# Tying VectorE, ScalarE and all of TensorE to source order through the first MLP's half units

## The chip, the cores and the metric

The kernel runs on one core of a Trainium2 chip. The time is the device time of one execution in microseconds (us); the number compared is the median over several executions.

## The reference, cut to what matters

The reference is a decoder trunk of two layers for 256 rows of width 2048 in float32. Layer 0 mixes with banded attention, layer 1 with a gated linear recurrence; each layer ends with a squared-ReLU MLP. Every sub-layer starts with an RMS norm, whose result is shifted and scaled by vectors that come from a conditioning vector c, and ends with a gated residual.

```python
def modulate(h, shift, scale):
    return h * (1.0 + scale[:, None, :]) + shift[:, None, :]
...
def swa_sink_attention(h, w_in, w_out, q_gain, k_gain, sinks):
    proj = h @ w_in
...
    return out.reshape(B, T, ATTN_Q_DIM) @ w_out
...
def squared_relu_mlp(h, w1, w2):
    a = jax.nn.relu(h @ w1)
    return (a * a) @ w2
```

The change reaches from the start of the kernel through layer 0's attention and through the first part of its MLP's up projection (2048 of 8192 columns). What follows, from the down projection of layer 0 to the end, is not touched by it.

## The kernel before, in words

**Weights.** All weights stream from memory in pieces of 1 MB, called raws (128 x 2048 float32), loaded by SyncE (L212) into a ring of five buffers (`NRAW`). `prep_one` (L225) handles the next raw of a list `seq` fixed in the source. There are three kinds. An "m" raw is one column block of the modulation weights: VectorE multiplies it with c and sums along the row (L233). A "g" raw is a quarter of a group of four such blocks, computed by TensorE (`gemv`). A "w" raw is a weight of a matrix product: it is split in two halves of 128 x 1024, each of which ScalarE casts to a rounded value `wh` (L250) and VectorE turns into the rest `wl` (L251). The halves have five buffers (`NW`).

**One unit.** A product is computed as high times high, low times high and high times low, in float32r. One "w" raw makes a unit of 16 x 3 matmuls of 256 columns, 48 in all. After each unit the source calls `ahead(LAG - 1)` (L309), which casts and splits the weight of the unit after the next one, with the "m" and "g" raws that stand before it in `seq`. A raw's buffer is loaded anew when its cast and split are done.

**The operands.** The left operand `h` or `o` of a product is made per block of 128 columns by `make_h` (L543): VectorE scales X into `ht` (L547), ScalarE adds the shift and rounds it (L551), VectorE makes the low part (L552). `mod_prep` (L531, L539) makes the scale `gsc` for it. `make_u` (L561) does the same without the norm and the shift (L564, L565 on ScalarE, L566 on VectorE).

**The stages of layer 0 here.** First the norm of X with its `gemv` matmuls for the first four shift blocks, then the first four `h`. Then the in projection of attention in four quarters (`mm_quarter`), each of which needs four more `h`; ten partial sums per quarter are copied out by ScalarE (L851 for the first quarter, L846 for the next two) and added up by GpSimd. In the fourth quarter the attention steps begin (`step`, L819): per-head norms of q and k go through a chain of small VectorE operations (`rsqrt`, L132 to L138), are widened by VectorE (`widen`, L662) and spread by TensorE (tile `rbk`). The out projection follows; residual units are added to X by L581.

**`open_mlp` (L882).** Its list `order` has eight residual units and then four that alternate with "u" units, then the last u units, eight u units in all. A u unit (`mm_uhalf`) multiplies the first eight blocks of X, not yet normed, with half of an up weight; its result is put into `part` (L926), its shift sums into `sums` (L925). In the meantime the squares of X are summed (L498, L499), and the norm comes out as `rbs`. Then the remaining eight operands are made (`more_h` in the loop over k), and a loop of eight p's runs the second half of the same weights: `mm_half(H, 1, ev)`, where `ev` scales `part` (L940), adds both halves (L948), applies squared ReLU (L967) and rounds the result (L476, L477), and `more_h(p, p + 1)` makes one more `h` for later. The results of all eight p's are the operands of the down projection.

**What sets the order.** The source's calls pass through Tile's scheduler, which places the instructions of each engine. Within an engine it may put them in another order than the source's. Only TensorE's calls go through the class `Queue` (L42); those made by `pep` are pinned, which means that each is tied behind the TensorE instruction that stands before it in the source. VectorE and ScalarE are plain engine objects. Work delayed by `later(n, ...)` is run by `hook` at the n-th slot after it in the source, with slots inside the units' matmul loops. On the chip an engine carries out its instructions in the order in which they were placed.

Of the kernel before, what the change touches and what calls it, by code (L numbers as in the profile page):

```python
# [41 lines left out]
class Queue:  # L42


    def __init__(self, tc, engine, last, pin):
        self.tc, self.engine, self.last, self.pin = tc, engine, last, pin

    def __getattr__(self, name):
        fn = getattr(self.engine, name)

        def call(*args, **kw):
            r = fn(*args, **kw)  # L52
            if self.pin and self.last:
                self.tc.add_manual_dep(
                    r.ins, self.last[-1],
                    mybir.DependencyInfo(mybir.DependencyClass.NoSync, mybir.DependencyReason.DATA),
                    reason="issue order")
            self.last[:] = [r.ins.name]
            return r
        return call  # L60
# [2 lines left out]
@with_exitstack  # L63
def trunk(ctx, tc, a, out):
    nc = tc.nc
    dve, act, sp, pool_q = nc.vector, nc.scalar, nc.sync, nc.gpsimd
    last = []
    pe, pep = Queue(tc, nc.tensor, last, False), Queue(tc, nc.tensor, last, True)

# [249 lines left out]
    def later(delay, fn):  # L319
        bg.append((bgst["slot"] + delay, bgst["n"], fn))  # L320
        bgst["n"] += 1
        bg.sort(key=lambda e: (e[0], e[1]))

    def hook():
        bgst["slot"] += 1
        while bg and bg[0][0] <= bgst["slot"]:
            bg.pop(0)[2]()
# [15 lines left out]
    def mm_std(op, evac, count=1, fold=False):  # L343
        keys = list(range(st["w"], st["w"] + count))
        ahead(count - 1)
        pss = [mmtile() for _ in keys]
        for kb in range(KB):
            while op[kb] is None:
                fill[0]()
            for i, key in enumerate(keys):  # L350
                wh, wl = wtile(key, kb)
                if fold:
                    three(pss[i][:, :T], wh, wl, op[kb], kb == 0, kb == KB - 1)
                else:
                    pe.matmul(pss[i], lhsT=wh, rhs=op[kb][:, :2 * T], start=(kb == 0), stop=False)
                    pe.matmul(pss[i][:, :T], lhsT=wl, rhs=op[kb][:, :T], start=False,
                              stop=(kb == KB - 1))
                if (kb * count + i) % 4 == 3:
                    hook()
        for i, key in enumerate(keys):  # L360
            evac(pss[i])
            W.pop(key)
        st["w"] += count
        ahead(LAG - 1, False)
# [102 lines left out]
    def wt(cols=T, name="w"):  # L467
        return tmp.tile([P, cols], F32, tag="w", name=name, bufs=3)
# [23 lines left out]
    def norm_add(kb):  # L492
        if kb == 0:
            nstate["ss"] = tmp.tile([P, T], F32, tag="rbs", name="ssum", bufs=1)
            act.activation(out=nstate["ss"], in_=X[kb], func=AF.Square)
            return
        sq = wt()
        act.activation(out=sq, in_=X[kb], func=AF.Square)  # L498
        dve.tensor_tensor(out=nstate["ss"], in0=nstate["ss"], in1=sq, op=ALU.add)  # L499

    def norm_rstd(sumcol=ones[:, :1]):
        ss = psum.tile([P, 2], F32, tag="sp", name="sst", bufs=2)
        for b in range(2):
            pe.matmul(ss[:, b:b + 1], lhsT=nstate["ss"][:, b * P:(b + 1) * P], rhs=sumcol,
                      start=True, stop=True)
        sm = tmp.tile([P, 8], F32, tag="nsm", name="nsm")
        dve.tensor_scalar(out=sm[:, 0:2], in0=ss, scalar1=1.0 / D, scalar2=EPS,
                          op0=ALU.mult, op1=ALU.add)
        rsqrt(sm[:, 0:2], sm[:, 2:4], sm[:, 4:6], sm[:, 6:8])
        dg = tmp.tile([P, T], F32, tag="dg", name="dg", bufs=1)  # L510
        for b in range(2):
            dve.tensor_scalar(out=dg[:, b * P:(b + 1) * P], in0=ident, scalar1=sm[:, 2 + b:3 + b],
                              scalar2=None, op0=ALU.mult)
        nstate["dg"] = dg

    def norm_bcast():
        rb = psum.tile([P, T], F32, tag="sp", name="rb", bufs=2)
        pe.matmul(rb, lhsT=ones, rhs=nstate["dg"], start=True, stop=True)
        rbs = tmp.tile([P, T], F32, tag="rbs", name="rbs", bufs=1)
        act.copy(out=rbs, in_=rb)  # L520
        return rbs
# [21 lines left out]
    def make_h(l, half, rbs, kb, s):  # L543
        sh = SH1 if half == 0 else SH2
        g = l * 2 + half
        t = tmp.tile([P, T], F32, tag="ht", name="ht", bufs=2)
        dve.scalar_tensor_tensor(out=t, in0=X[kb], scalar=gsc[:, g, kb:kb + 1], in1=rbs,  # L547
                                 op0=ALU.mult, op1=ALU.mult)
        shc = mods[:, l, sh * 16 + kb: sh * 16 + kb + 1]
        h = optile(sets[s], kb)  # L550
        act.activation(out=h[:, :T], in_=t, func=AF.Identity, bias=shc)  # L551
        dve.scalar_tensor_tensor(out=h[:, T:2 * T], in0=t, scalar=shc, in1=h[:, :T].bitcast(F32),  # L552
                                 op0=ALU.add, op1=ALU.subtract)
        return h
# [29 lines left out]
    def evac_res(l, which, n):  # L584
        def f(ps):
            resid(l, which, n, ps)
            finish_x(n)
        return f
# [3 lines left out]
    def finish_x(n):  # L592
        if ustate["next"] is not None and n < ustate["lim"]:
            ustate["U"][n] = make_u(*ustate["next"], n)
        if n < KB - 1:
            later(2, lambda: norm_add(n))
        elif ustate["next"] is None:
            norm_add(n)
# [283 lines left out]
    def open_mlp(mp, A, relu2):  # L882
        for n in range(4):
            finish_x(n)
        parts, H, box = [], [None] * KB, {}
        sums = mp.tile([P, KB], F32, tag="sums", name="sums")

        def more_h(k0, k1):
            for k in range(k0, k1):
                H[k] = make_h(0, 1, box["rbs"], k, 0)  # L890

        def s2():
            box["rbs"] = norm_bcast()

        def s1():
            norm_rstd()
            later(NB, s2)

        def s0():
            norm_add(KB - 1)  # L900
            later(1, s1)

        def res(n):
            mm_std(O, evac_res(0, G1, n), fold=True)
            if n == KB - 1:
                later(1, s0)

        for i, (kind, n) in enumerate(order):
            if i == NO:
                prep_mods(0, SC2, KH)  # L910
                prep_mods(0, SH2, KH)
                mod_prep(0, 1, 0, KH)
                start_u(0, 1, KH)
                U = ustate["U"]
                for k in range(KH):
                    U[k] = make_u(0, 1, k)
            if kind == "o":
                res(n)
                continue
            part = mp.tile([P, 2 * T], F32, tag=f"acc{n}", name=f"part{n}")  # L920
            parts.append(part)

            def keep(u, ps):
                c = 2 * n + u
                dve.tensor_reduce(out=sums[:, c:c + 1], in_=ps[:, T:T + 2], axis=AX.X, op=ALU.add)  # L925
                act.copy(out=part[:, u * T:(u + 1) * T], in_=ps[:, :T])  # L926
            mm_uhalf(U, keep)
        while "rbs" not in box:
            hook()
        ustate["next"], ustate["lim"] = None, KB  # L930
        sets.reverse()
        for k in range(KH, KB, 2):
            prep_mods(0, SC2, k + 2)
            prep_mods(0, SH2, k + 2)
            mod_prep(0, 1, k, 2)
            more_h(k, k + 2)
        ahead(LAG - 1, False)
        for p in range(8):
            t2 = wt(2 * T)
            dve.tensor_tensor(out=t2.rearrange("p (a b) -> p a b", b=T),  # L940
                              in0=parts[p].rearrange("p (a b) -> p a b", b=T),
                              in1=box["rbs"].unsqueeze(1).to_broadcast([P, 2, T]), op=ALU.mult)

            def ev(ps):
                for u in range(2):
                    t = t2[:, u * T:(u + 1) * T]
                    n = 2 * p + u
                    dve.scalar_tensor_tensor(out=t, in0=ps[:, u * T:(u + 1) * T], scalar=sums[:, n:n + 1],  # L948
                                             in1=t, op0=ALU.add, op1=ALU.add)
                    relu2(A, n, t)  # L950
            mm_half(H, 1, ev)
            more_h(p, p + 1)
        return H

    def mlp_layer(l, H, last):
# [399 lines left out]
```

## Time and profile before

| | us |
|---|---|
| median of 3 executions | 2356.22 |
| lowest and highest | 2351.72, 2356.53 |
| the profiled execution | 2348.51 |
| its span | 2346.7 |

The profiled execution has 1.8 us around its span and lies 7.7 us below the median. Times inside it are counted from the span's start. The first 42 us are setup and the first norm, 42 to 173 us the first three quarters of attention's in projection, 173 to 333 us the fourth quarter, the attention and the start of its out projection, 333 to 451 us the residual and u units of `open_mlp`, 451 to 497 us its loop over p; from 497 us on the down projection runs. In rows of the profile, all TensorE instructions carry the line of the `Queue` class (L52), so they are told apart by the tile's name: `mm` is a product's accumulator, `rbk` the spread norm of q and k, `gt` the turned `gemv` result. A row of the timeline gives start, duration, engine, line, operation and names; a figure in brackets at its end is the idle time before it and what ended it.

### The profile page before, as it was taken

The numbers are of one execution on the slowest core, as the hardware profiler recorded it, in microseconds if no ns is written. First come the engines' busy times: TensorE is split into PE (matmuls) and PEld (weight loads), VectorE is DVE, ScalarE is ACT, GpSimd is POOL, SyncE is SP. The second block draws the span as 40 slices with busy tenths as digits, with TensorE's granted clock in tenths as the row PEclk, the third lists the DMA queues.
The fourth block names the chain that finished last, engine by engine and source line by source line (L and its number), as shares of the span: only waits on it lengthen the run. The fifth ranks groups of instructions, "written<-read, shape, count | busy, mean of one in ns | idle before, by whom it ended". The sixth has DMA issues, their size and how long they took to land.

```text
span 2346.7 us, 37064 instructions
## 1 busy us (share of the span) xinstructions
PE 2269.6 (97%) x14690; PEld 1992.0 (85%) x14690; DVE 1788.2 (76%) x2908; ACT 1163.1 (50%) x1962; POOL 100.7 (4%) x94
## 2 busy tenths in 40 slices
PE   5887899999999999999999999999999999999999
PEld 3775579998888888888888898899888888888888
DVE  5668679975888898897998888767865766665665
ACT  3344454544444444455666666655544444444443
POOL 0133530000000000000000000000000000000000
PEclk8999999999999999999999999999999999999999
DMA  9886799756898899985577777645666666655552
GB/s 361 310 305 257 272 335 341 253 195 215 323 336 323 327 333 324 334 317 187 196 284 267 259 267 268 214 164 180 231 233 231 236 227 239 207 189 186 191 194 94
DMA packets 84638, 598.80 MB, mean 255 GB/s; under 512 B 9457, under 2 KB 11505, under 8 KB 12273
## 3 DMA queue, kind: packets, MB, share of 16 engines
q1 hardware_dynamic: 81936, 593.81, 70.3%
q8 instruction: 115, 1.88, 0.3%
q10 hardware_dynamic: 2304, 2.10, 0.3%
q0 software_dynamic: 224, 0.52, 0.1%
q14 instruction: 59, 0.48, 0.1%
HBM read 594.04 MB, written 2.10 MB: 254 GB/s over the span
## 4 chain that ended last, share of the span: by engine, by line
PE 92%; DVE 4%; ACT 2%; DMA 1%; issue 1%; POOL 0%; ACTq 0%; SPq 0%; DVEq 0%; POOLq 0%
PE mm L52 89%; ACT wh L250 1%; DVE raw L233 1%; PE A L52 1%; DVE wl L251 1%; PE on L52 0%; PE S L52 0%; POOL h L771 0%; DVE asm L751 0%; DMA raw<-in_aoutk_dram 0%; DMA raw<-in_mod_w_dram 0%; PE cb L52 0%; PE pt L52 0%; DVE h L552 0%; PE pv L52 0%
## 5 line engine op out<-in xcount | busy, mean ns | idle before, releaser
L251 DVE TENSOR_TENSOR wl<-raw,wh 128x1024 fp32r<-128x1024 f32 x744 | 909.3, 1226 | 429.7 <-ACT wh L250 427.9
L250 ACT CAST wh<-raw 128x1024 fp32r<-128x1024 f32 x744 | 778.4, 1050 | 850.9 <-PE mm L52 773.2
L52 PE MATMUL mm<-h,wh 128*128 128x512 f32 (+2 forms) x3728 | 1155.4, 368 | 35.1 <-ACT wh L250 34.6
L52 PE MATMUL mm<-h,wl 128*128 128x256 f32 (+1 forms) x3232 | 908.9, 282 | 1.5 <-DVE wl L251 1.4
L52 PE MATMUL mm<-o,wh 128*128 128x512 f32 (+2 forms) x3120 | 860.4, 346 | 0.2 <-ACT h L759 0.2
L52 PEld LDWEIGHTS mm<-h,wh 128*128 128x128 f32 x3728 | 671.5, 190 | 161.9 <-ACT wh L250 39.0
L52 PE MATMUL mm<-o,wl 128*128 128x256 f32 (+1 forms) x2432 | 679.2, 280 | 0.0
L52 PEld LDWEIGHTS mm<-h,wl 128*128 128x128 f32 x3232 | 612.2, 190 | 11.1 <-issue 3.4
L52 PEld LDWEIGHTS mm<-o,wh 128*128 128x128 f32 x3120 | 539.9, 189 | 82.3 <-issue 2.5
L52 PEld LDWEIGHTS mm<-o,wl 128*128 128x128 f32 x2432 | 457.9, 188 | 0.7 <-issue 0.3
L233 DVE CUSTOM_DVE_ANT_0 raw<-raw,cond 128x2048 f32<-128x2048 f32 x160 | 365.7, 2286 | 9.5 <-DMA raw<-in_mod_w_dram 9.3
L52 PE MATMUL mm<-wh,h 128*128 128x256 f32 x576 | 105.9, 283 | 4.2 <-DVE h L552 2.7
L52 PEld LDWEIGHTS mm<-wh,h 128*128 128x128 f32 x576 | 88.8, 188 | 8.0 <-DVE h L552 3.2
L52 PE MATMUL mm<-wl,h 128*128 128x256 f32 x288 | 81.0, 281 | 0.0
L472 ACT COPY w<-mm 128x256 f32<-128x256 f32 x186 | 68.1, 366 | 0.0
L771 POOL TENSOR_SCALAR h<-h,asm 128x128 f32<-128x128 f32 x64 | 64.6, 1027 | 69.7 <-DVE asm L754 21.1
L476 ACT CAST h<-w 128x256 fp32r<-128x256 f32 x125 | 49.8, 403 | 23.9 <-DVE w L967 23.0
L52 PEld LDWEIGHTS mm<-wl,h 128*128 128x128 f32 x288 | 54.3, 188 | 0.5 <-issue 0.4
L967 DVE SCALAR_TENSOR_TENSOR w<-w 128x256 f32<-128x256 f32 x125 | 52.0, 421 | 2.2
L477 DVE TENSOR_TENSOR h<-w,h 128x256 fp32r<-128x256 f32 x125 | 51.5, 417 | 0.0
L473 DVE TENSOR_TENSOR w<-mm,w 128x256 f32<-128x256 f32 x109 | 45.6, 418 | 0.4 <-ACT w L472 0.2
L988 DVE TENSOR_TENSOR acc<-mm,acc 128x256 f32<-128x256 f32 x96 | 40.5, 422 | 6.3 <-PE mm L52 3.8
(203 smaller groups left out, 1134.6 us busy)
## 6 DMA issues: line engine op xcount, KB each, us to landing
raw<-in_mod_w_dram SPq DMA_DIRECT2D x160, 1024.0 KB, 5.5
raw<-in_mlp_dram SPq DMA_DIRECT2D x128, 1024.0 KB, 4.9
raw<-in_hin_dram SPq DMA_DIRECT2D x64, 1024.0 KB, 5.0
raw<-in_mlp1b_dram SPq DMA_DIRECT2D x64, 1024.0 KB, 4.8
raw<-in_mlp1a_dram SPq DMA_DIRECT2D x48, 1024.0 KB, 5.2
raw<-in_mod_g_dram SPq DMA_DIRECT2D x32, 1024.0 KB, 6.1
raw<-in_ainq_dram SPq DMA_DIRECT2D x20, 1024.0 KB, 6.8
raw<-in_m1h_dram SPq DMA_DIRECT2D x16, 1024.0 KB, 5.1
```

Of the source, the lines that this page charges most:

```text
L52: r = fn(*args, **kw)
L233: dve.tensor_tensor_reduce(out=r, in0=r, in1=cond, scale=1.0, scalar=0.0, op0=ALU.mult, op1=ALU.add, accum_out=mods[:, e[1], e[2]:e[2] + 1])
L250: act.copy(out=wh, in_=part)
L251: dve.tensor_tensor(out=wl, in0=part, in1=wh.bitcast(F32), op=ALU.subtract)
L472: act.copy(out=t, in_=ps[:, T:])
L473: dve.tensor_tensor(out=out_t, in0=ps[:, :T], in1=t, op=ALU.add)
L476: act.copy(out=opt[:, :T], in_=src_t)
L477: dve.tensor_tensor(out=opt[:, T:2 * T], in0=src_t, in1=opt[:, :T].bitcast(F32), op=ALU.subtract)
L771: pool_q.tensor_scalar(out=Ls[hh][:, cut[b]], in0=Ls[hh][:, cut[b]], scalar1=ri[:, i:i + 1], scalar2=None, op0=ALU.mult)
L967: dve.scalar_tensor_tensor(out=t, in0=t, scalar=0.0, in1=t, op0=ALU.max, op1=ALU.mult)
L988: dve.tensor_tensor(out=acc[n], in0=ps[:, :T], in1=acc[n], op=ALU.add)
```

## The change

`Queue` gets a class flag `strict`. While it is set, every instruction called through a `Queue`, pinned or not, is tied behind the instruction that its own engine got before it from the source, by a dependency that sets the order only and adds no semaphore. VectorE and ScalarE now are `Queue` objects of their own, so the rule holds for them, too. The flag is set at the start of the trunk and cleared at the end of `open_mlp`, that is, before layer 0's down projection; from there on the scheduler places as before.

```diff
 class Queue:
+    strict = True
...
         def call(*args, **kw):
             r = fn(*args, **kw)
-            if self.pin and self.last:
+            if (self.pin or Queue.strict) and self.last:
                 self.tc.add_manual_dep(
...
 def trunk(ctx, tc, a, out):
     nc = tc.nc
-    dve, act, sp, pool_q = nc.vector, nc.scalar, nc.sync, nc.gpsimd
+    sp, pool_q = nc.sync, nc.gpsimd
+    Queue.strict = True
+    dve, act = Queue(tc, nc.vector, [], False), Queue(tc, nc.scalar, [], False)
...
             mm_half(H, 1, ev)
             more_h(p, p + 1)
+        Queue.strict = False
         return H
```

No instruction of the computation is added or taken away. GpSimd's and SyncE's orders are the same before and after; those of TensorE, VectorE and ScalarE differ. In the changed kernel all three engines' instructions carry the line of the class (L54).

**ScalarE in the first quarter.** `CAST wh<-raw` rows are the two halves of one unit's weight, `o_328` to `o_332` the copies of that quarter's partial sums out of `mm`. Before:

```order
L250 CAST wh<-raw 128x1024 x2
L851 COPY o_328<-mm 128x512
L250 CAST wh<-raw 128x1024 x2
L851 COPY o_329<-mm 128x512
L851 COPY o_330<-mm 128x512
L851 COPY o_331<-mm 128x512
L250 CAST wh<-raw 128x1024 x2
L851 COPY o_332<-mm 128x512
```

After:

```order
L54 CAST wh<-raw 128x1024 x4
L54 CAST distb<-w 128x128
L54 CAST distb<-w 128x256
L54 CAST identb<-cst 128x128
L54 COPY o_328<-mm 128x512
L54 COPY o_329<-mm 128x512
L54 CAST wh<-raw 128x1024 x2
L54 COPY o_330<-mm 128x512
L54 COPY o_331<-mm 128x512
L54 CAST wh<-raw 128x1024 x2
```

Two units' casts stand ahead of the first copy now instead of one, and the third unit's ahead of the second unit's copies instead of behind them: the casts run one unit further ahead.

**VectorE between the u units and the loop over p.** `sums<-mm` belongs to the last u units, `ht` and `o_4658`, `o_4663` are the first two of the eight operands for the loop. Before:

```order
L925 TENSOR_REDUCE sums<-mm 128x1
L251 TENSOR_TENSOR wl<-raw,wh 128x1024
L925 TENSOR_REDUCE sums<-mm 128x1
L547 SCALAR_TENSOR_TENSOR ht<-x_75,gsc,rbs 128x256
L251 TENSOR_TENSOR wl<-raw,wh 128x1024
L552 SCALAR_TENSOR_TENSOR o_4658<-ht,mods,o_4658 128x256
L547 SCALAR_TENSOR_TENSOR ht<-x_75,gsc,rbs 128x256
L251 TENSOR_TENSOR wl<-raw,wh 128x1024
L925 TENSOR_REDUCE sums<-mm 128x1
L251 TENSOR_TENSOR wl<-raw,wh 128x1024
L552 SCALAR_TENSOR_TENSOR o_4663<-ht,mods,o_4663 128x256
```

After:

```order
L54 TENSOR_REDUCE sums<-mm 128x1 x2
L54 TENSOR_TENSOR wl<-raw,wh 128x1024 x2
L54 TENSOR_TENSOR mods<-mods,cst 128x2 x2
L54 SCALAR_TENSOR_TENSOR gsc<-mods,cst 128x2
L54 SCALAR_TENSOR_TENSOR ht<-x_75,gsc,rbs 128x256
L54 SCALAR_TENSOR_TENSOR o_4658<-ht,mods,o_4658 128x256
L54 SCALAR_TENSOR_TENSOR ht<-x_75,gsc,rbs 128x256
L54 SCALAR_TENSOR_TENSOR o_4663<-ht,mods,o_4663 128x256
L54 TENSOR_TENSOR mods<-mods,cst 128x2 x2
L54 SCALAR_TENSOR_TENSOR gsc<-mods,cst 128x2
```

The operands were spread among the last u units; now all eight stand behind the last u unit's sums and its pair of `wl`, one after the other.

**VectorE in the loop over p.** One turn: `part` scaled into `w`, both halves of `mm` added, squared ReLU, the low parts `h`, the weight's `wl` pair and one `more_h`. Before, from p = 3:

```order
L940 TENSOR_TENSOR w<-part_4302,rbs 128x512
L948 SCALAR_TENSOR_TENSOR w<-mm,sums,w 128x256 x2
L967 SCALAR_TENSOR_TENSOR w<-w 128x256 x2
L251 TENSOR_TENSOR wl<-raw,wh 128x1024
L477 TENSOR_TENSOR h_4834<-w,h_4834 128x256
L477 TENSOR_TENSOR h_4839<-w,h_4839 128x256
L547 SCALAR_TENSOR_TENSOR ht<-x_74,gsc,rbs 128x256
L251 TENSOR_TENSOR wl<-raw,wh 128x1024
L940 TENSOR_TENSOR w<-part_4389,rbs 128x512
L552 SCALAR_TENSOR_TENSOR o_5158<-ht,mods,o_5158 128x256
```

After, from p = 0:

```order
L54 TENSOR_TENSOR w<-part_3900,rbs 128x512
L54 SCALAR_TENSOR_TENSOR w<-mm,sums,w 128x256
L54 SCALAR_TENSOR_TENSOR w<-w 128x256
L54 TENSOR_TENSOR h_4758<-w,h_4758 128x256
L54 SCALAR_TENSOR_TENSOR w<-mm,sums,w 128x256
L54 SCALAR_TENSOR_TENSOR w<-w 128x256
L54 TENSOR_TENSOR h_4763<-w,h_4763 128x256
L54 TENSOR_TENSOR wl<-raw,wh 128x1024 x2
L54 SCALAR_TENSOR_TENSOR ht<-x_73,gsc,rbs 128x256
L54 SCALAR_TENSOR_TENSOR o_4778<-ht,mods,o_4778 128x256
L54 TENSOR_TENSOR w<-part_4034,rbs 128x512
```

Each `h` now stands right behind the `w` from which ScalarE makes its rounded half, and each `o` right behind its `ht`; before, other work stood between.

## The prediction

> **What bounds the kernel now.** The page's first line comes first: TensorE is busy for 97% of the span of 2346.7 us, VectorE for 76%.
>
> ```profile
> PE 2269.6 (97%) x14690; PEld 1992.0 (85%) x14690; DVE 1788.2 (76%) x2908; ACT 1163.1 (50%) x1962; POOL 100.7 (4%) x94
> ```
>
> Second, the table of windows for the stages that the change reaches (start:end; busy time of TensorE, its weight loads, VectorE, ScalarE, GpSimd; granted clock; share of DMA; GB/s).
>
> ```profile
> 0.00:42.00 42.00, 18.24 (x85) 7.52 (x85) 21.94 (x71) 15.37 (x35) 0.87 (x5) 0.84 0.96 378
> 42.00:173.00 131.00, 110.73 (x805) 93.90 (x806) 81.81 (x97) 51.22 (x72) 29.10 (x18) 0.95 0.84 308
> 173.00:333.00 160.00, 136.53 (x1052) 97.30 (x1050) 122.91 (x318) 79.18 (x237) 70.15 (x70) 0.94 0.78 289
> 333.00:451.00 118.00, 117.49 (x985) 117.13 (x982) 107.71 (x173) 58.94 (x99) 0.00 (x0) 1.00 0.86 314
> 451.00:497.00 46.00, 46.00 (x390) 45.91 (x389) 43.28 (x81) 26.04 (x39) 0.00 (x0) 1.00 0.54 185
> ```
>
> TensorE has idle time to give back ahead of 333 us only. From 333 to 497 us it is full, and VectorE is busy for 91 to 94%: an order that makes VectorE wait costs time there. 390 matmuls in 46.0 us make 0.118 us for one, 5.66 for a unit of 48 and 2.83 for half a unit.
>
> Third, what TensorE waits for, in 42:173 (first row), 173:333 (second) and 333:497 (last): us in all, times, longest.
>
> ```profile
> PE mm L52 <- ACT wh L250: 19.7, 18, 1.9
> PE rbk L52 <- DVE w L662: 15.2, 4, 6.5
> PE mm L52 <- DVE wl L251: 0.5, 1, 0.5
> ```
>
> What the change can win lies in the first two rows, 34.9 us. The last says how little it can win behind 333 us.
>
> **Part by part.** Prices of VectorE's groups in 333:497, then ScalarE's (count; busy us, mean ns; idle time before):
>
> ```profile
> L251 DVE TENSOR_TENSOR wl<-raw,wh 128x1024 fp32r<-128x1024 f32 x56 | 67.3, 1218 | 4.3 <-ACT wh L250 4.2
> L233 DVE CUSTOM_DVE_ANT_0 raw<-raw,cond 128x2048 f32<-128x2048 f32 x15 | 34.3, 2284 | 0.0
> L581 DVE SCALAR_TENSOR_TENSOR x<-mm,mods,x 128x256 f32<-128x256 f32 x16 | 7.4, 479 | 2.0 <-PE mm L52 1.9
> L547 DVE SCALAR_TENSOR_TENSOR ht<-x,gsc,rbs 128x256 f32<-128x256 f32 x16 | 7.3, 475 | 0.0
> L552 DVE SCALAR_TENSOR_TENSOR o<-ht,mods,o 128x256 fp32r<-128x256 f32 x16 | 7.3, 476 | 0.0
> L948 DVE SCALAR_TENSOR_TENSOR w<-mm,sums,w 128x256 f32<-128x256 f32 x16 | 6.9, 473 | 1.2 <-PE mm L52 1.2
> L499 DVE TENSOR_TENSOR ssum<-ssum,w 128x256 f32<-128x256 f32 x15 | 6.3, 420 | 0.8 <-ACT w L498 0.8
> L940 DVE TENSOR_TENSOR w<-part,rbs 128x512 f32<-128x512 f32 x8 | 5.4, 679 | 0.0
> L477 DVE TENSOR_TENSOR h<-w,h 128x256 fp32r<-128x256 f32 x14 | 5.2, 411 | 0.0
> L967 DVE SCALAR_TENSOR_TENSOR w<-w 128x256 f32<-128x256 f32 x14 | 5.2, 410 | 0.0
> ```
>
> ```profile
> L250 ACT CAST wh<-raw 128x1024 fp32r<-128x1024 f32 x57 | 58.9, 1049 | 27.7 <-PE mm L52 23.5 <-issue 2.3 <-ACT o L551 1.7
> L551 ACT ACTIVATE o<-ht,mods 128x256 fp32r<-128x256 f32 x16 | 7.7, 507 | 0.8 <-DVE ht L547 0.8
> L564 ACT ACTIVATE h<-x,gsc 128x256 fp32r<-128x256 f32 x8 | 3.7, 496 | 0.0
> L926 ACT COPY part<-mm 128x256 f32<-128x256 f32 x16 | 5.9, 369 | 16.1 <-DVE sums L925 15.9
> L476 ACT CAST h<-w 128x256 fp32r<-128x256 f32 x14 | 5.2, 407 | 3.0 <-DVE w L967 3.0
> ```
>
> An instruction that follows another on its engine starts some 0.08 before the other's end, and a small one stays behind a long one ahead of it in the order, here 2.3 us behind a `wl` pair:
>
> ```profile
> 426.33 2.36 DVE L251 TENSOR_TENSOR wl<-raw,wh 128x1024 fp32r<-128x1024 f32 x2
> 428.61 0.15 DVE L136 TENSOR_TENSOR nsm<-nsm 128x2 f32<-128x2 f32 x1
> ```
>
> So each row counts its mean less 0.08 in a run of instructions. One operand then takes VectorE 0.40 (L547), a wait for ScalarE of 0.50 (L551) and 0.40 (L552): 1.30 in line, 0.80 if the wait is filled. `mod_prep` is three small operations, 0.45.
>
> *Setup: +5.* TensorE's first product starts its low part at 41.93; the last `gemv` matmuls end at 25.01.
>
> ```profile
> 23.97 1.04 PE mm L52 x8
> ...
> 26.81 2.20 DVE raw L233
> ...
> 41.93 15.31 PE mm L52 x110
> ```
>
> Now all 16 `gemv` matmuls (32 records of 0.13) follow the norm: 4.2 instead of 1.04, +3.1. Behind them VectorE does four L233 at 2.2, four operands at 1.30 and two `mod_prep`; with cast and `wl`, 17.2 instead of the 15.1 between 26.8 and 41.9: +2.1. Ring buffers also come free later: 3 to 8.
>
> *First three quarters: -15.* Casts a unit ahead no longer queue behind a copy that waits for TensorE, as here (3.27 us idle, then the pair of casts):
>
> ```profile
> 100.62 0.59 ACT L846 COPY w<-mm 128x512 f32<-128x512 f32 x1 [3.27 <-PE mm L52]
> 101.10 2.00 ACT L250 CAST wh<-raw 128x1024 fp32r<-128x1024 f32 x2
> ```
>
> That takes away up to the 19.7, and the clock of 0.95 becoming 1.00 gives up to 5% of 110.7, 5.5. Against it, at three quarter ends four operands and two `mod_prep` stand in one block, 4 x 1.30 + 2 x 0.45 = 6.1, of which half a unit, 2.83, hides: 3.3 each, 10 in all. The 39 raws of 1.05 MB at the first window's 378 GB/s need 108 us, so a window of 116 is possible. -20 to -5.
>
> *Fourth quarter and attention: -6.* The chain of small operations ahead of `widen` has been cut by long ones:
>
> ```profile
> 225.41 2.29 DVE L233 CUSTOM_DVE_ANT_0 raw<-raw,cond 128x2048 f32<-128x2048 f32 x1
> 230.12 1.22 DVE L251 TENSOR_TENSOR wl<-raw,wh 128x1024 fp32r<-128x1024 f32 x1
> 231.52 1.21 DVE L251 TENSOR_TENSOR wl<-raw,wh 128x1024 fp32r<-128x1024 f32 x1
> 233.58 1.94 PE L52 MATMUL rbk<-cst,w 128*128 128x128 f32 x8 [6.40 <-DVE w L662]
> ```
>
> In source order it is whole: 2.29 + 1.22 + 1.21 = 4.7 of a 6.40 wait go. The chain itself stays, so I take half of the 15.2, and give 2 back for softmax and `ssum` operations that now wait in line ahead of `wl`: -13 (nearly all of it) to +4 (none, and the waits double).
>
> *u units: +6.* `make_u` for eight blocks stands in one piece ahead of the next unit's split: ScalarE's 0.42 and a small cast of 0.1 for each set the pace, 4.2 and 0.6 around it. VectorE's work per unit behind TensorE (L581 0.40, L233 2.20, `wl` 2.36, L499 0.34, 5.3) nearly fills 5.66, so of this 4.8 only about 1 is made up: +3.6. The norm's sum waits for the last residual unit's L581, L233, `wl` pair and L499, 5.3, while TensorE has half a unit to do: +2.4. 2 to 10.
>
> *From the u units into the loop: +14.* Let T be the end of the last u unit on TensorE, 451 us before. VectorE has its sums, a copy (0.37), a cast (1.05) and a `wl` pair (2.36) with handoffs at T + 4.15, `mod_prep` at 4.6, the first operand at 5.9, seven more and three `mod_prep` at 5.9 + 9.1 + 1.35 = 16.35. TensorE then ends the first half unit: 0.36 for its last block, 2.83 for the weight's second half, T + 19.5 instead of 5.66. Nothing covers this: the unit needs all eight operands. 10 to 17.
>
> After such a gap the clock may be down; a spell in the quarters bounds it, pairs at 0.63 that take 0.40 at full clock:
>
> ```profile
> 60.33 0.40 PE L52 MATMUL mm<-h,wh 128*128 128x256 f32 x2
> 70.12 0.63 PE L52 MATMUL mm<-h,wh 128*128 128x256 f32 x2
> ```
>
> By these rows the second half's 2.83 could grow by 0.58 of itself, 1.6, which the range holds. The Trainium skill ("TensorE: Matmul & The Clock Gate", "What's actually happening") has the clock halve after an idle window of about 3.4 us; by it that half would take 2.8 more (an estimate from it), 2376 in all. The trace before has no gap of this kind at this place to decide it.
>
> *The loop over p: +13.* In line, a turn of VectorE is twice L948, L967, wait for L476, L477 (0.39 + 0.33 + 0.40 + 0.33 = 1.45), 0.60 till the cast behind them is done, the `wl` pair 2.28, one operand 1.30 and L940 0.65: 2.9 + 0.6 + 2.28 + 1.30 + 0.65 = 7.73, more than TensorE's 5.66. Seven turns from T + 19.5 begin the last at T + 73.6, and the second down unit's first `wl` is there 4.7 later, T + 78.3. Before, nine units end at T + 50.9. Of these 27.4 the row above has 13.8; 13.6 remain, 10 to 17. What hid the waits was the other work between them.
>
> *Sum.* 5 - 15 - 6 + 6 + 14 + 13 = +17. Behind the loop nothing differs. The profiled execution (2348.5) would become 2365.5; it lay 7.7 below the median, so I add 17 to 2356.2: **2373**.
>
> **The rivals.** Faster or slower by 0.2% (4.7 us) is about what a measurement of this kernel can tell from no change.
>
> A. *The early lead pays for the loop.* Everything ahead of 333 us runs a unit ahead: waits of 19.7 and 15.2 go and the clock's 5.5 comes, 40.4, the blocks at quarter ends being hidden. For it speaks that both waits are queueing behind other work; against it, VectorE's 6.1 blocks. With the lower ends behind 333 us and in setup (3 + 2 + 10 + 10) it gives -15: 2341. It decides if TensorE reaches the first residual unit over 33 us before 333, which is what the terms behind it cost, or over 22 with their lower ends.
>
> B. *Gains and losses cancel.* The quarters at -20, attention at -13, the rest at 5 + 4 + 12 + 12: 0, 2356. Speaks for it that both are of one size.
>
> C. *The early gain fails.* Blocks of 6.1 with nothing beside them cost the quarters 18, so -7, attention's waits give +2; with 5 + 7 + 16 + 15: +38, 2394. For it: DMA is at 84%, and raws come free only as VectorE reaches them.
>
> That the change does nothing is excluded: the orders of three engines differ.
>
> **How the numbers follow.** The forecast has 0.53 (2360 to 2388), A 0.17, B 0.10, C 0.20. Half of A and of C left out gives 2350 to 2396. Faster 0.18 (A and little else), same 0.09 (B), slower 0.73.
>
> **What would show it.** Right: the first product at 46 to 48 us; casts of `wh` hardly waited for in the quarters; `rbk` waits of about 7; a gap of TensorE of some 13 us with only one half of a unit in it at the end of the u units; turns of 7.7 us in the loop over p, and TensorE waiting for `wl` there. Wrong: the loop's turns stay near 5.7, or the lead at the first residual unit is over 22 us or below zero.

## The result and the profile after

The changed kernel takes 2405.45 us (median; 2404.04 to 2409.51) against 2353.97 before: both medians of four executions. The ratio is 1.0223, 95% interval 1.0201 to 1.0245: 51 to 53 us slower, with an interval of 47 to 58. The forecast was 2373, 17 slower; the range ended at 2396. The direction was right, and the size was a third of what it is.

The page's first line after. VectorE, ScalarE and TensorE have as many instructions as before. TensorE's 38.7 us more of busy time go with a lower granted clock, 0.975 instead of 0.990 over the span; what of them is the clock alone is not separated here.

```profile
PE 2308.3 (96%) x14690; PEld 2012.4 (84%) x14690; DVE 1800.8 (75%) x2908; ACT 1163.1 (48%) x1962; POOL 130.5 (5%) x94
```

To put the two traces beside each other, a stage must end at the same instruction in both. These marks serve: the first low part on TensorE (41.93 before), the end of the last GpSimd sum of the quarters, and the starts of the last `pv` matmul of the attention, of the last `sums` of the u units, and of the first and last addition of `mm` in the loop over p (L948). First before, then after; the figures behind the colon are durations in ns (least, median, most), then the first and last start.

```profile
177.84 1.79 POOL L847 TENSOR_TENSOR o<-o,w 128x512 f32<-128x512 f32 x1 [2.39 <-ACT w L846]
...
L52 PE MATMUL pv<-PT,vnat x128: 272/379/689, 224.2 to 332.8; 128*64 128x256 f32 x64, 128*64 128x128 f32 x64
...
L925 DVE TENSOR_REDUCE sums<-mm x16: 146/152/160, 389.1 to 451.2; 128x1 f32<-128x2 f32 x16
...
L948 DVE SCALAR_TENSOR_TENSOR w<-mm,sums,w x16: 462/472/487, 457.2 to 496.9; 128x256 f32<-128x256 f32 x16
```

```profile
49.10 0.58 PE L54 MATMUL mm<-h,wl 128*128 128x256 f32 x1 [0.47 <-DVE wl L54]
...
171.05 2.53 POOL L851 TENSOR_TENSOR o<-o,w 128x512 f32<-128x512 f32 x2 [7.94 <-ACT w L54]
...
L54 PE MATMUL pv<-PT,vnat x128: 272/326/676, 231.4 to 346.7; 128*64 128x256 f32 x64, 128*64 128x128 f32 x64
...
L54 DVE TENSOR_REDUCE sums<-mm x16: 149/154/160, 411.0 to 472.3; 128x1 f32<-128x2 f32 x16
L54 DVE SCALAR_TENSOR_TENSOR w<-mm,sums,w x16: 476/481/485, 494.5 to 556.8; 128x256 f32<-128x256 f32 x16
```

That gives the ledger, in us:

| stage | before | after | difference | predicted |
|---|---|---|---|---|
| setup, to the first low part on TensorE | 41.9 | 49.1 | +7.2 | +5 |
| three quarters | 137.7 | 124.5 | -13.2 | -15 |
| fourth quarter and attention | 153.2 | 173.1 | **+19.9** | **-6** |
| u units | 118.4 | 125.6 | +7.2 | +6 |
| way into the loop over p | 6.0 | 22.2 | +16.2 | +14 |
| loop over p, first to last L948 | 39.7 | 62.3 | **+22.6** | **+13** |
| the rest | 1849.8 | 1850.7 | +0.9 | 0 |

The sum is +60.8 between these two executions, and 51.5 between the medians: the profiled execution before lay 5.5 us below its median, and the one after, at 2409.5, is the slowest of its four. In nine of the experiments below the three quarters have the orders of before, and their profiles show 136.9 to 142.0 us for this stage; so a few us between two traces need not come from the change. Four of six stages came within 2.2 us of the forecast. The window table after, cut at the same marks, shows the two that did not, with the way into the loop between them, and what the clock did there (0.94 and 1.00 in about the same stages before):

```profile
173.60:346.70 173.10, 139.81 (x997) 95.27 (x997) 119.03 (x307) 73.14 (x229) 86.72 (x68) 0.89 0.66 245
...
472.30:494.50 22.20, 14.43 (x51) 10.50 (x51) 11.77 (x33) 6.32 (x11) 0.00 (x0) 0.62 0.22 88
494.50:556.80 62.30, 52.38 (x364) 48.95 (x362) 46.22 (x81) 22.99 (x36) 0.00 (x0) 0.92 0.34 118
```

In the attention stage, 10.3 of the 19.9 us are more idle time of TensorE (153.2 - 130.2 = 23.0 before, 173.1 - 139.8 = 33.3 after), and 9.6 more busy time at a lower granted clock, with 997 matmuls instead of 1000. TensorE's waits there: the wait for `rbk` is 7.1 instead of 15.2, as forecast, but one for `wh` has come that was not there.

```profile
PE mm L54 <- ACT wh L54: 7.4, 3, 5.3
PE rbk L54 <- DVE w L54: 7.1, 5, 3.1
```

The worst of it in TensorE's timeline: the last `gemv` matmuls beside a set of attention steps, then a wait, then the next unit, at first with slower matmuls.

```profile
209.77 1.06 PE L54 MATMUL mm<-raw,cst 128*32 128x512 f32 x8
216.13 0.80 PE L54 MATMUL mm<-h,wh 128*128 128x256 f32 x2 [5.29 <-ACT wh L54]
...
217.77 0.63 PE L54 MATMUL mm<-h,wh 128*128 128x256 f32 x2
...
224.13 0.40 PE L54 MATMUL mm<-h,wh 128*128 128x256 f32 x2
```

The 5.29 us of idle time are followed by pairs of 0.63 (granted clock 0.55 from 217.0 to 223.7), and those of 0.40 are back only at 224.1: one wait is paid twice, the second time as TensorE's busy time. ScalarE's timeline shows why the weight was late. `h<-S` rows are the exponentials of an attention step; this is the start of three steps, the end of the third, and the cast that TensorE waits for:

```profile
201.14 0.35 ACT L54 ACTIVATE h<-S,asm 128x128 f32<-128x128 f32 x1
...
208.12 0.35 ACT L54 ACTIVATE h<-S,asm 128x128 f32<-128x128 f32 x1
...
213.44 0.35 ACT L54 ACTIVATE h<-S,asm 128x128 f32<-128x128 f32 x1
...
214.93 0.21 ACT L54 ACTIVATION_READ_ACCUMULATOR h<-S,asm 128x1 f32 x1
215.03 2.00 ACT L54 CAST wh<-raw 128x1024 fp32r<-128x1024 f32 x2
```

The cast begins as soon as the third step's last row on ScalarE is done, and these steps wait in turn for VectorE's `asm`, 5.16 us ahead of the second and 3.51 ahead of the third.

### The profile page after: what moved, and what is told of

Read it like the earlier page. It is cut to its first block, busy times and chain, and to the rows that moved or that the text cites. A ratio compares the mean times of both kernels' runs of the same rounds, so it can differ in the third digit from the quotient of the medians.

```text
span 2407.5 us, 37054 instructions
## 1 busy us (share of the span) xinstructions
PE 2308.3 (96%) x14690; PEld 2012.4 (84%) x14690; DVE 1800.8 (75%) x2908; ACT 1163.1 (48%) x1962; POOL 130.5 (5%) x94
## 4 chain that ended last, share of the span: by engine, by line
PE 87%; DVE 7%; ACT 3%; DMA 1%; issue 1%; DVEq 0%; ACTq 0%
PE mm L54 84%; DVE wl L54 2%; DVE raw L54 1%; ACT wh L54 1%; DMA raw<-in_ainq_dram 1%; DVE w L54 1%; ACT h L54 1%; PE A L54 1%; DVE asm L54 1%; DVE h L54 1%; DVE ht L54 1%; DVE o L54 1%; PE S L54 1%; PE on L54 0%; DVE qw L54 0%
## 5 line engine op out<-in xcount | busy, mean ns | idle before, releaser
L54 DVE TENSOR_TENSOR wl<-raw,wh 128x1024 fp32r<-128x1024 f32 x744 | 912.3, 1234 | 414.7 <-ACT wh L54 411.9
L54 PE MATMUL mm<-h,wh 128*128 128x512 f32 (+2 forms) x3728 | 1167.8, 371 | 32.1 <-ACT wh L54 23.8
L54 ACT CAST wh<-raw 128x1024 fp32r<-128x1024 f32 x744 | 775.9, 1051 | 859.9 <-PE mm L54 750.5
L54 PE MATMUL mm<-h,wl 128*128 128x256 f32 (+1 forms) x3232 | 912.2, 283 | 3.2 <-DVE wl L54 3.2
L54 PE MATMUL mm<-o,wh 128*128 128x512 f32 (+2 forms) x3120 | 872.0, 349 | 13.2 <-ACT o L54 7.2
L54 PEld LDWEIGHTS mm<-h,wh 128*128 128x128 f32 x3728 | 678.4, 191 | 171.7 <-ACT wh L54 28.3
L54 PE MATMUL mm<-o,wl 128*128 128x256 f32 (+1 forms) x2432 | 683.9, 282 | 5.0 <-DVE wl L54 5.0
L54 PEld LDWEIGHTS mm<-o,wh 128*128 128x128 f32 x3120 | 546.5, 191 | 99.5 <-ACT o L54 10.2
L54 PEld LDWEIGHTS mm<-h,wl 128*128 128x128 f32 x3232 | 616.7, 191 | 5.0 <-DVE wl L54 4.6
L54 PEld LDWEIGHTS mm<-o,wl 128*128 128x128 f32 x2432 | 461.8, 190 | 6.8 <-DVE wl L54 6.4
L54 DVE CUSTOM_DVE_ANT_0 raw<-raw,cond 128x2048 f32<-128x2048 f32 x160 | 367.9, 2300 | 22.6 <-DMA raw<-in_mod_w_dram 22.5
L54 ACT COPY w<-mm 128x256 f32<-128x256 f32 (+1 forms) x308 | 118.3, 386 | 34.6 <-PE mm L54 34.6
L54 PE MATMUL mm<-wh,h 128*128 128x256 f32 x576 | 108.0, 287 | 3.1 <-DVE h L54 2.2
L54 PEld LDWEIGHTS mm<-wh,h 128*128 128x128 f32 x576 | 90.6, 192 | 7.5 <-DVE h L54 2.9
L775 POOL TENSOR_SCALAR h<-h,asm 128x128 f32<-128x128 f32 x64 | 84.6, 1337 | 68.3 <-DVE qw L54 25.0
L54 PE MATMUL mm<-wl,h 128*128 128x256 f32 x288 | 81.8, 284 | 0.0
L54 ACT CAST h<-w 128x256 fp32r<-128x256 f32 x125 | 50.4, 403 | 52.5 <-DVE w L54 51.5
L54 DVE TENSOR_TENSOR h<-w,h 128x256 fp32r<-128x256 f32 x125 | 52.4, 420 | 7.5 <-ACT h L54 7.5
L54 PEld LDWEIGHTS mm<-wl,h 128*128 128x128 f32 x288 | 55.4, 192 | 0.2
L54 DVE SCALAR_TENSOR_TENSOR w<-w 128x256 f32<-128x256 f32 x125 | 52.9, 423 | 2.8
L851 POOL TENSOR_TENSOR o<-o,w 128x512 f32<-128x512 f32 x20 | 42.3, 2127 | 111.4 <-ACT w L54 111.3
```

What stands on the lines that cost most here:

```text
L775: pool_q.tensor_scalar(out=Ls[hh][:, cut[b]], in0=Ls[hh][:, cut[b]], scalar1=ri[:, i:i + 1], scalar2=None, op0=ALU.mult)
L851: pool_q.tensor_tensor(out=parts[p], in0=parts[p], in1=t, op=ALU.add)
```

## Experiments

Each is the changed kernel with the edit shown; "tied" means that the flag is set. It starts set in e1 and e13 and cleared in the others. Medians of before in these series are 2349.8 to 2350.6.

### One stage at a time

Theory 1 is the ledger itself: each stage's difference is made in that stage, and they add up. The rivals are in the expectations.

**e1**, the three quarters with setup. Edit: the flag is cleared when the fourth quarter begins.

```diff
         for s_, fin_part in enumerate((first_part, add_part, add_part, done_part)):
+            if s_ == 3:
+                Queue.strict = False
```

> The order is tied from the start through the first three quarters of attention's in projection only, and free from the fourth quarter on. Theory 1 (the stages' losses add up as the two traces show them: setup +7 us, three quarters -12, fourth quarter and attention +19, u units +7, way into the loop over p +16.5, loop +21): 5 us faster than before, 2349. The prediction's ledger (+5, -15): 10 us faster, 2344. Rival (a stage that ends early is given back later, since TensorE then waits for raws that come no sooner): no change, within 3 us.

Measured: 2346.4, ratio 0.9981 (0.9971 to 0.9992), 4.5 us faster. Theory 1 holds in the sum. In the profile the parts are others: setup +6.1, the three quarters -16.1, and +6.2 in the fourth quarter and attention, where the order is free. So part of what the quarters win is given back, as the rival has it, though not all, and not by its reason: TensorE waits there for `rbk`, 21.4 us, and not for raws.

**e2**, the fourth quarter and attention alone: the flag starts cleared, is set where e1 clears it, and cleared at the top of `open_mlp`.

> Tied only from the fourth quarter to the end of the out projection's first part. Theory 1: +19 us, 2373. The prediction's ledger: -6, 2348. Rival (the attention loses in the changed kernel only because the quarters ahead of it left the ring of raws in another state): within 5 us of before.

Measured: 2367.9, ratio 1.0070 (1.0051 to 1.0089), 16.5 us slower (12 to 21). Theory 1 holds, the prediction's -6 falls, and so does the rival that blamed the state that the quarters leave.

**e3**, `open_mlp` alone: the flag is set at its top.

> Tied only in open_mlp (u units, way into the loop, loop over p). Theory 1: 7 + 16.5 + 21, +44 us, 2398. The prediction's ledger: 6 + 14 + 13, +33, 2387.

Measured: 2394.6, ratio 1.0180 (1.0161 to 1.0198), 42 us slower, as theory 1 has it. The three add up to -4.5 + 16.5 + 42 = 54, against the whole change's 51 to 53.

**e4**, its second part alone: the flag is set where the norm is known.

```diff
         while "rbs" not in box:
             hook()
+        Queue.strict = True
```

> Tied only from the point in open_mlp at which the norm is known: the eight operands and the loop over p. Theory 1: 16.5 + 21, +37 us, 2391. The prediction's ledger: 14 + 13, +27, 2381.

Measured: 2380.8, ratio 1.0124 (1.0107 to 1.0141), 29 us slower. This is less than theory 1's 37. Its profile has the first L948 17.7 us behind the last `sums` instead of 22.2, while the loop takes 62.3 as in the changed kernel; some of the way in is lost only when the u units ahead of it are tied too.

### Which engine's order

**e5 and e6**: as e2, with VectorE alone tied, and with ScalarE alone. The flag becomes the set of the queues that are tied:

```diff
-            if (self.pin or Queue.strict) and self.last:
+            if (self.pin or id(self.last) in Queue.strict) and self.last:
...
+            if s_ == 3:
+                Queue.strict = (id(dve.last),)
```

> Tied from the fourth quarter to the end of the out projection's first part, VectorE's instructions alone; ScalarE and TensorE stay with the scheduler. Theory 1 (VectorE in source order runs the L233 sums, the weight splits and the softmax reductions one after the other as they are written, so that TensorE has no product ready while an attention step is worked off): most of the 16.5 us that all three engines cost there, 12 or more. Theory 2 (the weight casts, which ScalarE in source order does only behind the exponentials of the steps, are what TensorE waits for): under 5 us.

> The same place, ScalarE's instructions alone. Theory 1: under 5 us. Theory 2: 12 us or more. If both singles are small and only the two together cost 16.5, neither theory holds alone.

Measured: VectorE alone 2365.5, ratio 1.0072 (1.0056 to 1.0088); ScalarE alone 2362.8, 1.0056 (1.0036 to 1.0076). Both theories fall as they were put: either engine alone costs most of the 16.5 (17 and 13 us), and the two do not add up. In both profiles TensorE waits for `wh`, 6.0 and 5.6 us. That either half of a weight is enough to hold it up, since a unit needs the cast and the split, fits this; it is argued, not shown by these two.

**e7 and e8**: as e4, with VectorE alone and ScalarE alone.

> Tied from the point at which the norm is known to the end of the loop over p, VectorE alone. Theory 1 (VectorE idles in line at each handoff to ScalarE and back: turns of 8.65 us, and the eight operands one after the other): nearly the 29 us of the three engines together, 24 or more. Theory 2 (ScalarE's casts of the weight, which in source order stand behind the rounding of this turn's results, come late): under 10.

> The same place, ScalarE alone. Theory 1: under 5 us. Theory 2: 15 or more.

Measured: VectorE alone 2391.9, ratio 1.0186 (1.0169 to 1.0203), 44 us slower; ScalarE alone 2357.6, 1.0030 (1.0013 to 1.0046), 7 slower (3 to 11). Theory 1 holds for VectorE, and more: with ScalarE and TensorE free, the tied VectorE does worse than with all three tied, and its turns take 10.20 us (508.75 to 518.95) instead of 8.64. For ScalarE alone theory 1's under 5 lies within the interval, and theory 2's 15 does not. In e7's profile ScalarE's row of a weight's cast stands ahead of the rounding that VectorE waits for in line (first ScalarE, then VectorE):

```profile
509.87 1.05 ACT L54 CAST wh<-raw 128x1024 fp32r<-128x1024 f32 x1 [2.35 <-PE mm L54]
510.82 0.40 ACT L54 CAST h<-w 128x256 fp32r<-128x256 f32 x1
```

```profile
509.26 0.42 DVE L54 SCALAR_TENSOR_TENSOR w<-w 128x256 f32<-128x256 f32 x1
511.25 0.43 DVE L54 TENSOR_TENSOR h<-w,h 128x256 fp32r<-128x256 f32 x1 [1.57 <-ACT h L54]
```

The wait is 1.57, where it is 0.47 with ScalarE in source order too; in the loop such waits add up to 22.4 us in e7 and to 6.6 in e4. So VectorE's order without slack was here only as good as ScalarE's order matched it. That TensorE is free as well in e7 was not tested apart.

### What the time is made of

**e9**: e4, with the loop written in another source order. Operands are written in pairs (`half_h` scales one and gives its rounding and its low part as two calls, `scaled` multiplies the next `part`), and the turn becomes:

```diff
-                for u in range(2):
...
-                    dve.scalar_tensor_tensor(out=t, in0=ps[:, u * T:(u + 1) * T], scalar=sums[:, n:n + 1],
-                                             in1=t, op0=ALU.add, op1=ALU.add)
-                    relu2(A, n, t)
+                for u in range(2):
...
+                    dve.scalar_tensor_tensor(out=ts[u], in0=ps[:, u * T:(u + 1) * T],
+                                             scalar=sums[:, n:n + 1], in1=ts[u], op0=ALU.add, op1=ALU.add)
+                for t in ts:
+                    dve.scalar_tensor_tensor(out=t, in0=t, scalar=0.0, in1=t, op0=ALU.max, op1=ALU.mult)
+                for u in range(2):
...
+                    act.copy(out=A[2 * p + u][:, :T], in_=ts[u])
+                hi, lo = half_h(p)
+                for u in range(2):
+                    dve.tensor_tensor(out=A[2 * p + u][:, T:2 * T], in0=ts[u],
...
+                    nt[0] = scaled(p + 1)
+                hi()
+                box["lo"] = lo
             mm_half(H, 1, ev)
-            more_h(p, p + 1)
+            box["lo"]()
```

> e4 with another source order: the eight operands are written in pairs (both scalings, both roundings, both low parts), and in the loop over p both halves go through each operation together, the next operand's scaling and the next part's scaling stand where VectorE waited for ScalarE, and the operand's low part stands behind the weight split. Theory 1 (the loss is idle handoff time in line, not the tie as such): turns fall from 8.65 us to about 6, eight of them give back some 20 us, the pairs some 5; of e4's +29 us 4 to 10 are left, 2358. Rival (a tied VectorE is late because all eight operands stand behind the last u unit, and the loop only repeats that lateness): turns stay over 8 and +24 or more is left.

Measured: 2364.5, ratio 1.0060 (1.0045 to 1.0076), 14 us slower, where 4 to 10 were expected; of e4's 29, 15 are gone. VectorE's turn before (first and last row: the same place one turn apart), after, and in e9:

```profile
479.61 0.86 DVE L948 SCALAR_TENSOR_TENSOR w<-mm,sums,w 128x256 f32<-128x256 f32 x2
480.40 0.74 DVE L967 SCALAR_TENSOR_TENSOR w<-w 128x256 f32<-128x256 f32 x2
...
485.13 0.88 DVE L948 SCALAR_TENSOR_TENSOR w<-mm,sums,w 128x256 f32<-128x256 f32 x2
```

```profile
494.48 0.48 DVE L54 SCALAR_TENSOR_TENSOR w<-mm,sums,w 128x256 f32<-128x256 f32 x1 [4.12 <-PE mm L54]
494.99 0.42 DVE L54 SCALAR_TENSOR_TENSOR w<-w 128x256 f32<-128x256 f32 x1
495.89 0.43 DVE L54 TENSOR_TENSOR h<-w,h 128x256 fp32r<-128x256 f32 x1 [0.47 <-ACT h L54]
496.23 0.48 DVE L54 SCALAR_TENSOR_TENSOR w<-mm,sums,w 128x256 f32<-128x256 f32 x1
...
498.60 2.36 DVE L54 TENSOR_TENSOR wl<-raw,wh 128x1024 fp32r<-128x1024 f32 x2 [0.52 <-ACT wh L54]
500.87 0.48 DVE L54 SCALAR_TENSOR_TENSOR ht<-x,gsc,rbs 128x256 f32<-128x256 f32 x1
501.93 0.48 DVE L54 SCALAR_TENSOR_TENSOR o<-ht,mods,o 128x256 fp32r<-128x256 f32 x1 [0.58 <-ACT o L54]
...
503.12 0.48 DVE L54 SCALAR_TENSOR_TENSOR w<-mm,sums,w 128x256 f32<-128x256 f32 x1
```

```profile
488.88 0.87 DVE L54 SCALAR_TENSOR_TENSOR w<-mm,sums,w 128x256 f32<-128x256 f32 x2
489.66 0.75 DVE L54 SCALAR_TENSOR_TENSOR w<-w 128x256 f32<-128x256 f32 x2
...
492.32 2.36 DVE L54 TENSOR_TENSOR wl<-raw,wh 128x1024 fp32r<-128x1024 f32 x2 [0.24 <-ACT wh L54]
...
494.99 0.87 DVE L54 SCALAR_TENSOR_TENSOR w<-mm,sums,w 128x256 f32<-128x256 f32 x2
```

Turns take 5.52, 8.64 and 6.11. The waits in brackets of the middle one (0.47, a second 0.47 further down, 0.52, 0.58) are gone in e9 but for one of 0.24, as theory 1 has it; the rival's turns of over 8 did not come. The way in stayed longer than I expected: 13.7 in e9's profile, from the last `sums` (456.8) to the first L948 (470.5), against 6.0 before and 17.7 in e4, because the eight operands still stand behind the last u unit. Of the 14 us that are left this makes 7.7, and the loop 3.6 (43.3 instead of 39.7).

**e11**: e2, with the "m" and "g" raws of the fourth quarter listed one weight later, so that the next unit's weight is prepared ahead of the three attention steps.

```diff
-        per=lambda i: (0, 0, 0, 6, 12, 18, 22, 26, 32)[i])
+        per=lambda i: (0, 0, 0, 0, 6, 12, 18, 22, 26)[i])
```

> e2 with the modulation raws of the fourth quarter and the out projection listed one weight later, so that the next unit's weight is cast and split ahead of the three attention steps and not behind them. Theory 1 (TensorE waits there for a weight that stands behind the steps: 10.1 us on wh, and a slow clock after it): of e2's +16.5 us 3 to 7 are left. Rival (the steps' own chains on VectorE, with the L233 sums between them, set the stage): 13 or more are left.

Measured: 2357.3, ratio 1.0025 (1.0009 to 1.0040), 6 us slower; 10.5 of the 16.5 are gone. TensorE's longest wait in e2's attention, and in e11's:

```profile
PE mm L54 <- ACT wh L54: 10.1, 3, 7.8
```

```profile
PE rbk L54 <- DVE w L54: 7.6, 5, 3.1
```

In e11 no wait for `wh` is left, and that for `rbk` is as in e2 (7.1). The cast now stands ahead of the three steps (197.47, the first step's exponentials at 210.33), while VectorE does an L233 in each of the three steps as it did in e2. Between the marks of the ledger the attention takes 156.9 us in e11's profile, 171.6 in e2's and 153.2 before. So the attention's loss was mainly the weight behind the steps; the chains of the norms were not. What makes the remaining 3.7 there (6 by the medians) stays open; the longest wait of TensorE's that before does not have is one of 2.9 us ahead of `ssq`.

### What the change is worth where it wins

**e10**: e1 without setup; the flag is set where the quarters' loop begins.

> Tied in the three quarters alone: as e1, but setup and the first norm are free as before. Theory 1 (setup's +5 to +7 is a loss of its own): 9 to 11 us faster than before. Rival (what setup loses is made up in the quarters, or the quarters' gain is given back in the attention whenever it comes): as e1, 4.4 faster.

Measured: 2338.4 (2336.0 to 2339.8), ratio 0.9953 (0.9940 to 0.9965): 11 us faster than before. Theory 1's figure came, and this kernel is faster than both of the two compared. Its last `pv` is at 322.8 instead of 332.8, and in the attention behind it `rbk` is waited for more than before (15.2), for a reason that no run here separates:

```profile
PE rbk L54 <- DVE w L54: 22.2, 5, 6.5
```

How the loss of setup reaches the end is not as theory 1 put it: in the traces e1's first low part comes 5.0 us behind e10's, its quarters end only 1.3 behind (169.67 against 168.34), and its last `pv` is 6.3 behind (329.1), though both are free from the fourth quarter on.

**e12**: e10 with e11's list.

> e10 with e11's list: the three quarters tied, everything behind free, the raws of the fourth quarter listed one weight later. Theory 1 (a free order has hidden that weight already, as TensorE's waits for it in e10's attention are nil): as e10, 11 to 12 us faster than before, within 3. Rival (VectorE's long instructions ahead of the norms' chains move out of their way): 15 or more faster.

Measured: 2341.0, ratio 0.9960 (0.9946 to 0.9975), 9 us faster (6 to 13). As theory 1 has it: in this free order the list changes nothing that the measurement can tell.

**e13**: TensorE alone tied, from the start to the first norm's end.

> TensorE alone tied, in setup and the first norm only, so that all gemv matmuls stand behind the norm's; VectorE is free and, in its new order, does the first L233 sum ahead of the result it waits for. If the setup's loss (e1 against e10, 7 us) is TensorE's order, 4 us or more slower than before. If it takes a tied VectorE that sits in line behind that result, 2 us or less.

Measured: 2354.7, ratio 1.0026 (1.0012 to 1.0039), 6 us slower (3 to 9). By the figure this is TensorE's order; the trace says otherwise about the place:

```profile
28.80 0.66 PE L54 MATMUL gt<-cst,w 128*128 128x128 f32 x4 [0.72 <-ACT w L54]
...
42.93 0.58 PE L54 MATMUL mm<-h,wl 128*128 128x256 f32 x1 [0.46 <-DVE wl L54]
```

`gt` comes 3.1 later than before, as worked out, but the first low part only 1.0, because VectorE does an L233 in the meantime. The rest of what this profile has more lies in the three quarters, 141.8 us instead of 137.7, at a granted clock of 0.87 instead of 0.96 from 100 to 140 us. The orders there are those of before. e6, e8, e9 and e11, which leave setup and the quarters free too (one `gemv` matmul of setup stands a place earlier than before), have 141.6 to 142.0 and the same 0.87; e2 to e5 and e7 have 136.9 to 137.1 and 0.96. So these 4 us come without any tie of setup, and with TensorE alone tied the trace leaves 1.0 to setup. In the changed kernel `gt` reaches VectorE 5.0 us later than before, and VectorE then needs 2.1 more to the first low part (31.41 to 49.10 against 26.37 to 41.93):

```profile
26.37 0.17 DVE L273 TENSOR_REDUCE mods<-gt 128x4 f32<-128x16 f32 x1 [3.15 <-PE gt L52]
```

```profile
24.31 5.70 PE L54 MATMUL mm<-raw,cst 128*32 128x512 f32 x32
...
31.41 0.17 DVE L54 TENSOR_REDUCE mods<-gt 128x4 f32<-128x16 f32 x1 [8.31 <-PE gt L54]
```

So `gt` comes late by TensorE's order, and it costs its whole delay where VectorE is tied and idles for it (8.31 us); VectorE tied alone in setup was not run.

## Why the prediction was wrong

**Setup, +5 against +7.2.** Right in mechanism and nearly in size: VectorE's line cost the 2.1 that were forecast, and the `gemv` matmuls behind the norm 5.0 and not 3.1, since the 32 of them took 5.70 and not 4.2. e1 is slower than e10 by 6 to 7 us.

**Three quarters, -15 against -13.2.** Right in its main term: of the 19.7 us of waits for `wh` there is no row left after the first product. That the sum came so near is luck in part. The clock, which was to rise from 0.95 to 1.00 and give 5.5, was 0.92, and the blocks at quarter ends, which were to cost 10, show as 5.2 of waits for operands; the two misses cancel. TensorE's idle time fell by 12.9, its busy time by 0.3. e10 shows the gain alone: 11 us.

**Attention, -6 against +19.9 in the traces and +16.5 in e2.** This is the step that failed. It read: "In source order it is whole: 2.29 + 1.22 + 1.21 = 4.7 of a 6.40 wait go", and gave only 2 us back for work that now waits in line. The first half came true; `rbk` is waited for 7.1 instead of 15.2. The second half looked at what stands in line ahead of the norms, and not at what those steps now stand ahead of: the same three long instructions, an L233 and the weight splits, stood between the small ones, and the next unit's weight was ready in time: before, TensorE has no wait for `wh` there. In source order its cast and split come behind three attention steps; TensorE waits for them, and then works more slowly for a while. e11 gives 10.5 of the 16.5 back by preparing that weight ahead of the steps, and by nothing else. The range's upper end for this term, +4, took no account of a weight behind the steps; the row to use was the quarters' own wait, `wh` behind other work.

**u units, +6 against +7.2.** Right in the sum, and in the norm's wait: 2.5 for `ssum`, where 2.4 were forecast. The eight blocks of `make_u` cost less than the 3.6 put down: TensorE starts 0.35 late and takes 4.24 for them (401.65 to 405.89), where eight blocks at 0.36 take 2.88. A spell of slow pairs behind the norm's wait (444.96 to 448.18), which the sum did not have, adds about 1.4.

**The way into the loop, +14 against +16.2.** Right. Two operands and a `mod_prep` take 3.38 (the starts of the two rows), where I had 2 x 1.30 + 0.45 = 3.05, about 1 us in all:

```profile
477.69 1.10 PE L54 MATMUL mm<-o,wh 128*128 128x256 f32 x2 [5.39 <-ACT o L54]
481.07 1.10 PE L54 MATMUL mm<-o,wh 128*128 128x256 f32 x2 [0.61 <-ACT o L54]
...
489.29 5.16 PE mm L54 x27
```

The last row of this chain is the last block and the weight's second half: 27 matmuls in 5.16, where 0.36 + 2.83 = 3.19 were counted. So the low clock, which I had kept in the range at 1.6, cost 2.0. By the half rate of the Trainium skill ("TensorE: Matmul & The Clock Gate", "What's actually happening") it would have cost 2.8, an estimate from that page for the whole second half. The trace has the slow spell for the first part alone: pairs take 0.63 up to 491.7 and 0.40 from 492.9 on.

**The loop, +13 against +22.6.** The mechanism was right: turns are longer than a unit, and TensorE waits for the weight (from 472.3 to 557 us 5.1 for `wh`, 4.5 for `wl`). The size of a turn was not, 8.64 instead of 7.73. I had taken 0.08 off every duration, as between rows that follow one another. That holds for independent instructions: two L948 take 0.86, and the next begins 0.79 after the first. But L967 reads what the addition ahead of it wrote, and it begins 0.51 after the start of a 0.48 operation. In line, nearly every instruction depends on the one before, so each half costs 1.75 and not 1.45, the operand 1.46 and not 1.30. So this step failed in the size of its turn. From the first L948 to the last there are seven turns; at 0.91 more each they make 6.4 of the 9.6. The rest is mostly that the forecast counts to the second down unit's first `wl`, and the ledger to the last L948: by the forecast's own ends it has 58.8 us, and the trace 65.9 (494.5 to 560.4), 7.1 more.

**The sum.** By the traces, 26 us of the miss are the attention (22 to 23 by e2's median) and 10 the loop; the median missed the forecast by 32. Of the two signs of being wrong that were named, one came: the lead at the first residual unit is below zero, with the last `pv` 13.9 us later than before. Rival C came nearest (2394), but for a reason that did not come: the quarters' blocks cost no 18 us.

## What to carry to other kernels

Before tying an engine's order, list for each long instruction that the scheduler had moved forward who waits for it next; what it was put in front of was the smaller half of the account here (8.1 us of `rbk` waits won, 10.5 lost by the weight). In this kernel the tie paid where the source already writes work a unit ahead, as in the quarters (e10); the stages with handoffs between engines are better left to the scheduler, or partly filled by hand (e9). The price of an instruction in a dependent line is its start-to-start time from a dependent line, not its duration less an overlap.

## What the runs showed of the hardware

GpSimd's normalising of the probabilities, 64 instructions of the same shapes, took 1027 ns each on average before and 1337 in the changed kernel. The rows name one shape, but there are two, 32 instructions of each: 876 and 1318 ns for 128x128, 1178 and 1356 for 128x256.

```profile
L771 POOL TENSOR_SCALAR h<-h,asm 128x128 f32<-128x128 f32 x64 | 64.6, 1027 | 69.7 <-DVE asm L754 21.1 <-DVE qw L136 18.9 <-DVE asm L752 18.2
```

```profile
L775 POOL TENSOR_SCALAR h<-h,asm 128x128 f32<-128x128 f32 x64 | 84.6, 1337 | 68.3 <-DVE qw L54 25.0 <-DVE asm L54 20.5 <-ACT asm L54 11.9
```

What stands beside them on VectorE differs, and no run here was made to separate this. The 128x128 ones take 1205 to 1313 in e2, e5 and e11, where VectorE is tied in the attention, and 822 to 990 in e1, e3, e9, e10 and e12, where no engine is; the profile's spans on GpSimd are rough. In e11 TensorE waits for them only once, 1.5 us.

A slow spell of TensorE can outlast the wait ahead of it: after 5.29 us of idle time it worked from 216.1 to 223.7 with hardly a gap before its pairs were back at 0.40.
